# A hybrid decoder layer on one core: the output weights of cross-attention loaded into the queries' input room, the mixer's constants spread by DMA, the attention heads' buffers taken by the parity of the pair

## The chip, the core and the metric

The kernel runs on one core of one Trainium2 chip. A core has a matrix engine (PE, TensorE), three engines for elementwise work (DVE or VectorE, ACT or ScalarE, POOL or GpSimd) and SP (SyncE), which in this kernel only issues DMA transfers. Each engine carries out its own list of instructions in order and waits on semaphores for the others. The metric is the device time of one execution in microseconds, the median of several. The time includes a little before the first and after the last recorded instruction, so it is somewhat longer than the span of the trace.

## What is computed

One layer of a decoder over 1024 positions of 1024 channels, in float32, with three sub-layers. The reference, cut to its frame:

```python
h = rms_norm(x, g_pre_mix)
q, k, v, z, xbc, dt_raw, ga, gs = split(h @ w_in, IN_SIZES)
o_att = stick_breaking_attention(q, k, v)         # 16 heads of 64
o_ssm = ssd_branch(z, xbc, dt_raw, ...)           # Mamba-2: 32 heads of 64, 4 groups, state 128, chunks of 128
merged = sigmoid(ga) * (o_att @ w_br_att) + sigmoid(gs) * (o_ssm @ w_br_ssm)
x = x + rms_norm(merged @ w_mix_out, g_post_mix)
h = rms_norm(x, g_pre_xa)
mem_n = rms_norm(mem, g_mem)                      # 256 external memory rows
x = x + rms_norm(memory_cross_attention(h, mem_n, w_xq, w_xkv, w_xo), g_post_xa)   # 4 heads of 256
h = rms_norm(x, g_pre_ffn)
x = x + rms_norm(swiglu(h, w_gu, w_down), g_post_ffn)   # 2816 hidden
```

Stick-breaking attention weights position s for position t by exp(z_ts + the sum of log sigmoid(-z_tj) over j from s to t); the mixer's decays inside a chunk are exp of differences of a running sum a_cs, and 0 above the diagonal. The last product of cross-attention, `@ w_xo` with its norm and residual, is one of the two places that the change touches.

## The kernel before

**Numbers in two parts.** The matrix engine works here on a rounded float32 (fp32r). Each operand is therefore split into a high part (hi_sb, lines 88 to 97: a copy with rounding, on POOL by L93 or on ACT by L97, where no engine is named the two in turn) and a low part (lo_of, L99: what is left after subtracting the high part, L100, on DVE or POOL). Each product is three matmuls (mm3, L102 to 106): high by high (L103), high by low (L104), low by high (L105). A weight must so be loaded, rounded on one engine and subtracted on another before PE may use it.

**Stages.** In order of time: input projection; stick-breaking attention with the projections of its heads in between (to about 1080 us); the SSD mixer, with the memory's key and value projections mixed in; the two branch projections and the mixer's output projection; cross-attention; its output projection (1763 to 1890 us); the feed-forward layer and its down projection. A scheduler lays down each engine's order when the program is built, from the order in which the code asks for things, the free rooms of the buffer pools and its own idea of durations. What counts here is that the order on each engine is fixed: an instruction that waits holds all behind it on its engine, on SP too, where all DMA transfers stand in one list.

**Attention's end.** Heads are handled in pairs, hp from 0 to 7. ev_q and ev_k store the projected queries and keys of a pair into one tile per head, `qk` (queries, high keys, low keys), from a ring of four rooms: a new pair's two tiles take the rooms of the pair two earlier. PE computes scores (L867 to 883) into which DVE runs a scan (L882); then, for the values (L889 to 931), PE transposes the weights into one of three PSUM banks `tr` (L898), ACT makes their high part `wth` (L901), DVE the low part `wtl` (L902), which frees the bank, and PE multiplies both with the values (L910, L911). DVE multiplies the result with its gate (oT, L919), and SP stores it (o_d, L921) and a gate (g_d, L859).

**The memory.** While the last pairs are at work, SP loads the memory's gain (L1194) and its two blocks of 128 rows (L1199) into `wraw` tiles, a pool of three; ACT squares a block (L1201), POOL turns the mean into 1/root (rstd, L166 and L167), DVE normalises (L1202), and PE transposes (L1209). The `wraw` rooms are then used by the weights of the memory's keys and values (two_loads, L1218 to 1229, load L1225), high part on ACT, low part on DVE. These tiles lie in memory that attention's tiles had before, so the first of them wait for the last user of that memory.

**The mixer's decays.** A decay matrix of a chunk is one matmul (dec, L1077) of a row of `colrows` (128 x 8 heads x 128) with `keyrows` (128 x 512), followed by an exp on ACT (L1078). Rows 0 to 7 and 32 to 39 of both hold the heads' sums in two parts and the ones that select a head, rows 64 and 65 the sums of the columns; the others hold FAR = -2^120 times the identity against a mask of zeros and ones, so that what lies above the diagonal becomes exp of a huge negative number. There are two `colrows` and two `keyrows`, used in turn. What is constant in them is built once by DVE (L1015 to 1025): 128x1024 from the identity, then three narrow strips and two blocks of 8 rows for each `colrows`, and a copy of the mask for each `keyrows`. Of these sixteen, twelve go through `slow`, which pins each behind one of the last fourteen matmuls of the values, so that they are spread over attention's end. The sums that change from chunk to chunk are then loaded from DRAM: keyrows (L1033, called key_d below), colrows (L1070, sum_d), and the inputs xs (L1072).

**Cross-attention's output.** big_weight (L1334) loads a 1024x1024 weight in eight rows of tiles `raw` and makes eight tiles `bw`. Its `raw` tiles come from a ring of two `wraw` rooms, so a load waits until the low part of the weight two before it has been taken. For w_xo it is called on L1698 with npool = 2: the first two weights are done on POOL alone, the others get their high part by turns on POOL and ACT and their low part on DVE. out_proj (L1401) then runs over four row blocks, for each over the eight weights, into a PSUM tile `p`, one of two; ACT squares the result (L1417), DVE normalises it (L1419) and adds the residual (L1420). Cross-attention's queries are made from four `a8` tiles (128 x 2 x 1024) in the pool accp, which the queries' projection reads last; the same pool takes the FFN's input `hf` afterwards.

## Time and profile before

| what | us |
|---|---|
| median of 3 runs | 2546.85 (2546.82 to 2547.27) |
| the profiled execution's own time | 2547.56 |
| span of its trace | 2545.8 |
| mean granted clock of PE over the span | 0.995 |

The stages, from the busy table by stretch (PE's busy time):

| stretch, us | what runs | PE busy | share |
|---|---|---|---|
| 0 to 375 | input projection, first part | 356.9 | 95% |
| 375 to 680 | input projection, second part | 303.1 | 99% |
| 680 to 1080 | attention | 391.3 | 98% |
| 1080 to 1490 | mixer, memory's projections, first branch work | 394.4 | 96% |
| 1490 to 1760 | branch and output projections, cross-attention | 267.0 | 99% |
| 1760 to 1890 | cross-attention's end and its output projection | 126.5 | 97% |
| 1890 to 2546 | feed-forward, down projection | 635.9 | 97% |

A busy share is read as what is left over: where PE is busy for 97% of a stretch, 3% of it is all that other engines and transfers take from it, unless the granted clock is below 1, when the same matmuls take longer. In the rows quoted below, the columns of a list of single instructions are: start (us), length (us), engine, line, operation, written tile <- read tiles with shapes, count, and in brackets the idle time before it and what ended it. "SPq" is the instruction queue of SP, where a row is the issue of a transfer and not the transfer. A row of the list of waits gives engine, tile and line, then what ended the wait, then sum, count and longest in us.

### The profile page before, as it was taken

Reading aid. Unit: us, or ns where it says so; the run is one execution under the profiler, and the core shown is the slowest. Engines: PE = TensorE matmul, PEld = TensorE weight load, DVE = VectorE, ACT = ScalarE, POOL = GpSimd, SP = SyncE. Lnnn points to the kernel's source line nnn. Section 1 sums busy time; section 2 is a strip of 40 time slices with the busy share of each in tenths; the row PEclk is TensorE's granted clock in tenths of the full one; section 3 lists DMA queues with packets and bytes.
Section 4 is the critical chain, followed back from the end, with each engine's and each line's share of the span. In section 5 each row is a group of like instructions: output and inputs, shape, how many; then the busy total and the mean of one; then the engine's idle time right before and its main releaser. Section 6 shows DMA issues by size and latency. Waiting matters only on the chain. (4 is left out here: it accounts for less than half of the span.)

```text
span 2545.8 us, 32843 instructions
## 1 busy us (share of the span) xinstructions
PE 2475.0 (97%) x12002; PEld 2054.4 (81%) x12002; DVE 1858.3 (73%) x2205; ACT 1153.8 (45%) x2068; POOL 793.2 (31%) x632
## 2 busy tenths in 40 slices
PE   8999999999999999998999999999999999999998
PEld 6788788888888888787888788888787888887776
DVE  7685888776788887697888554576459666666997
ACT  6343455655555655565554302344233333334433
POOL 4331533321000000165655131131113233223675
PEclk9999999999999999999999999999999999999999
DMA  6441565445444454364332452311231322324322
GB/s 229 150 155 59 156 205 174 141 133 165 115 124 119 116 129 104 113 201 154 106 96 77 152 166 87 127 48 58 100 124 59 97 78 75 99 84 165 132 100 100
DMA packets 284524, 310.02 MB, mean 122 GB/s; under 512 B 17343, under 2 KB 204872, under 8 KB 283978
## 3 DMA queue, kind: packets, MB, share of 16 engines
q1 hardware_dynamic: 284362, 307.91, 39.0%
q8 instruction: 95, 1.56, 0.3%
q14 instruction: 67, 0.55, 0.1%
HBM read 206.26 MB, written 78.52 MB: 112 GB/s over the span
## 5 line engine op out<-in xcount | busy, mean ns | idle before, releaser
L882 DVE TENSOR_TENSOR_SCAN n<-n,mask 128x128 f32<-128x128 f32 (+7 forms) x128 | 170.7, 1349 | 37.9 <-ACT n L881 37.3
L199 POOL TENSOR_TENSOR sf<-wr,wr 128x512 f32<-128x512 f32 x38 | 59.3, 1561 | 351.1 <-DMA wr<-in_w_gu_dram 131.0
L100 DVE TENSOR_TENSOR sw<-sf,sw 128x512 fp32r<-128x512 f32 x150 | 116.3, 786 | 53.8 <-ACT sw L97 53.4
L93 POOL TENSOR_SCALAR whi<-wraw 128x1024 fp32r<-128x1024 f32 x10 | 18.4, 1836 | 398.5 <-PE mm L104 324.3
L97 ACT ACTIVATE sw<-sf 128x512 fp32r<-128x512 f32 x150 | 91.9, 624 | 95.1 <-PE mm L225 85.5
L881 ACT ACTIVATE n<-sc 128x512 f32<-128x512 f32 (+1 forms) x192 | 87.0, 493 | 93.3 <-PE sc L880 92.9
L225 PE MATMUL mm<-h,sw 128*128 128x512 f32 x320 | 124.3, 389 | 1.8 <-DVE sw L100 1.8
L97 ACT ACTIVATE sw<-wr 128x512 fp32r<-128x512 f32 x113 | 70.9, 629 | 121.0 <-PE mm L225 120.9
L223 PE MATMUL mm<-h,sw 128*128 128x512 f32 x320 | 122.4, 391 | 3.1 <-ACT h L97 2.3
L224 PE MATMUL mm<-h,sw 128*128 128x512 f32 x320 | 124.5, 389 | 0.0
L902 DVE SCALAR_TENSOR_TENSOR wtl<-tr,wth 128x512 fp32r<-128x512 f32 x192 | 99.5, 545 | 30.5 <-ACT wth L901 30.2
L901 ACT ACTIVATE wth<-tr,mone 128x512 fp32r<-128x512 f32 x192 | 106.6, 583 | 26.2 <-PE tr L898 24.1
L166 POOL TENSOR_SCALAR rstd<-ms 128x1 f32<-128x1 f32 x82 | 33.5, 409 | 262.6 <-ACT x L1417 101.8
L670 DVE SCALAR_TENSOR_TENSOR b<-b,prmT,b 128x1023 f32<-128x1023 f32 (+2 forms) x72 | 102.8, 1430 | 9.4 <-ACT b L668 8.9
L100 DVE TENSOR_TENSOR sw<-wr,sw 128x512 fp32r<-128x512 f32 x113 | 93.1, 827 | 18.9 <-ACT sw L97 18.8
L103 PE MATMUL mm<-oth,bw 128*128 128x512 f32 x256 | 103.6, 405 | 2.3 <-DVE a L1188 1.5
L898 PE MATMUL tr<-ident,n 128*128 128x128 f32 x576 | 98.7, 276 | 5.7 <-DVE wtl L902 5.7
L103 PE MATMUL p<-bw,h 128*128 128x512 f32 x256 | 99.4, 393 | 3.3 <-DVE x L1419 2.4
L105 PE MATMUL mm<-oth,bw 128*128 128x512 f32 x256 | 100.9, 394 | 0.0
L105 PE MATMUL p<-bw,h 128*128 128x512 f32 x256 | 100.5, 393 | 0.0
L104 PE MATMUL mm<-otl,bw 128*128 128x512 f32 x256 | 100.5, 393 | 0.0
L104 PE MATMUL p<-bw,h 128*128 128x512 f32 x256 | 100.4, 392 | 0.0
(695 smaller groups left out, 8182.6 us busy)
## 6 DMA issues: line engine op xcount, KB each, us to landing
wr<-in_w_gu_dram SPq DMA_DIRECT2D x80, 256.0 KB
wr<-in_w_in_dram SPq DMA_DIRECT2D x36, 512.0 KB
zr<-in_w_in_dram SPq DMA_DIRECT2D x32, 512.0 KB
gu_d<-t SPq DMA_DIRECT2D x44, 256.0 KB
qk<-hT SPq DMA_DIRECT2D x84, 128.0 KB
qk<-lT SPq DMA_DIRECT2D x84, 128.0 KB
wraw<-in_w_in_dram SPq DMA_DIRECT2D x20, 512.0 KB
b<-v_d SPq DMA_DIRECT2D x16, 512.0 KB
```

The source lines that it names most:

```text
L97: A.activation(o, i, AF.Copy)
L100: eng.tensor_tensor(o, i, hi.bitcast(F32), ALU.subtract)
L103: first = T.matmul(ps, sh, mh, start=start, stop=False)
L104: T.matmul(ps, sh, ml, start=False, stop=False)
L105: T.matmul(ps, sl, mh, start=False, stop=stop)
L223: T.matmul(ps, w[0][:, k, :], b[0][:, k, :], start=first and k == 0, stop=False, skip_group_check=True)
L224: T.matmul(ps, w[0][:, k, :], b[1][:, k, :], start=False, stop=False, skip_group_check=True)
L225: T.matmul(ps, w[1][:, k, :], b[0][:, k, :], start=False, stop=last and k == 3, skip_group_check=True)
L670: V.scalar_tensor_tensor(acc[:, sh:], y[:, :S - sh], cw(3 - sh, f), acc[:, sh:], ALU.mult, ALU.add)
L882: V.tensor_tensor_scan(nt[:, 0:L][:, ::-1], nt[:, 0:L][:, ::-1], mask[:, S - L:][:, ::-1], 1.0, ALU.mult, ALU.max)
L901: A.activation(wh[:, t0 * P:], pt[:, t0 * P:], AF.Identity, bias=mone)
L902: V.scalar_tensor_tensor(wl[:, t0 * P:], pt[:, t0 * P:], -1.0, wh[:, t0 * P:].bitcast(F32), ALU.add, ALU.subtract)
```

## The change

Three edits.

1. The heads' tiles `qk` come from two rings of two, `qk0` for even pairs and `qk1` for odd ones, in place of one ring of four. The room is the same.
2. The constants of the decays are no longer built in full by DVE. DVE makes one 128x128 tile `base` (four operations on at most 128x128), a DMA spreads it over the eight heads of colrows[0], DVE writes the two blocks of eight rows, a DMA copies colrows[0] into colrows[1], and two DMAs copy the mask into the two keyrows. Nothing of it is pinned any more.
3. big_weight can take its `raw` tiles from another pool. For w_xo these are the four `a8` tiles of accp, two weights in each, so that all eight loads have a room of their own. The six weights that POOL does not do alone now all get their high part on ACT.

```diff
--- before.py
+++ after.py
@@ -821,7 +821,7 @@
                     for j in range(2):
                         hd = heads[2 * hp + j]
                         if half == 0:
-                            t = mk(qk, [P, 3, S], F32R, "qk")
+                            t = mk(qk, [P, 3, S], F32R, f"qk{hp % 2}", bufs=2)
                             hd["q"], hd["kh"], hd["kl"] = [t[:, i] for i in range(3)]
                         q = hd["q"]
                         rows_ = slice(j * HD, (j + 1) * HD)
@@ -1002,26 +1002,21 @@
         HEADS, ONES = (0, 32), 64
         colrows = [mk(ep, [P, GH, P], F32R, f"colrows{i}") for i in range(NROW)]
         keyrows = [mk(ep, [P, HALF], F32R, f"keyrows{i}") for i in range(2)]
-        spread = iter(marks[-14:])
-
-        def slow(ins):
-            m = next(spread, None)
-            if m is not None:
-                issue_behind(ins, m)
-
+        base = mk(ep, [P, P], F32, "base")
+        V.tensor_scalar(base, ident, FAR, None, ALU.mult)
+        for r, n in ((0, GH), (32, GH), (ONES, 2)):
+            V.tensor_scalar(base[:, r:r + n], ident[:, r + n:r + n + 1].to_broadcast([P, n]), FAR, None, ALU.mult)
         u = mk(sm, [P, 4, P], F32, "cb")
         G.memset(u, 1.0)
         G.affine_select(u, u, [[0, 4], [1, P]], ALU.is_gt, 0.0, base=0, channel_multiplier=-1)
-        for t in colrows:
-            slow(V.tensor_scalar(t, ident.unsqueeze(1).to_broadcast([P, GH, P]), FAR, None, ALU.mult))
-            for r, n in ((0, GH), (32, GH), (ONES, 2)):
-                ins = V.tensor_scalar(t[:, :, r:r + n], ident[:, r + n:r + n + 1].unsqueeze(1).to_broadcast([P, GH, n]), FAR, None, ALU.mult)
-                if r != 32:
-                    slow(ins)
-            for r in HEADS:
-                slow(V.tensor_copy(t[r:r + GH], ident[r:r + GH, r:r + GH].unsqueeze(2).to_broadcast([GH, GH, P])))
+        t = colrows[0]
+        nc.sync.dma_start(t.bitcast(F32), base.unsqueeze(1).to_broadcast([P, GH, P]))
+        for r in HEADS:
+            V.tensor_copy(t[r:r + GH], ident[r:r + GH, r:r + GH].unsqueeze(2).to_broadcast([GH, GH, P]))
+        for i in range(1, NROW):
+            nc.sync.dma_start(colrows[i].bitcast(F32), t.bitcast(F32))
         for t in keyrows:
-            slow(V.tensor_copy(t, u.rearrange("p c i -> p (c i)")))
+            nc.sync.dma_start(t.bitcast(F32), u.rearrange("p c i -> p (c i)"))
             G.memset(t[ONES:ONES + 2].bitcast(F32), 1.0)
 
         def open_four(g, q):
@@ -1331,18 +1326,23 @@
 
 
 
-    def big_weight(wb, w, npool=0, rooms=()):
+    def big_weight(wb, w, npool=0, rooms=(), raws=None):
         wh, wl = [], []
         first = {}
         for k in rooms:
             first[k] = mk(wb, [P, D], F32, "wraw", bufs=2) if k is None else mk(wb, [P, 2, D], F32R, f"bw{k}", bufs=1)
         for k in range(KT):
-            raw = first.pop(None) if None in first else mk(wb, [P, D], F32, "wraw", bufs=2)
+            if raws is not None:
+                if k % 2 == 0:
+                    two = mk(raws, [P, 2, S], F32, "a8")
+                raw = two[:, k % 2]
+            else:
+                raw = mk(wb, [P, D], F32, "wraw", bufs=2)
             nc.sync.dma_start(raw, w[k * P:(k + 1) * P, :])
             both = first[k] if k in first else mk(wb, [P, 2, D], F32R, f"bw{k}", bufs=1)
             wh.append(both[:, 0, :])
             wl.append(both[:, 1, :])
-            hi_sb(wh[k], raw, "p" if k < npool else None)
+            hi_sb(wh[k], raw, "p" if k < npool else ("a" if raws is not None else None))
             lo_of(wl[k], raw, wh[k], G if k < npool else V)
         return wh, wl
 
@@ -1695,7 +1695,7 @@
     with ExitStack() as q3:
         gpool = pool(q3, "gx3")
         wbig = pool(q3, "wbigB", 8, side="right")
-        wxo = big_weight(wbig, a["w_xo"][0], 2, (7, 6, 5, 4, 3, None, 0, 1, 2))
+        wxo = big_weight(wbig, a["w_xo"][0], 2, (7, 6, 5, 4, 3, None, 0, 1, 2), accp)
         gpost, gpre = load_gain(gpool, "g_post_xa"), load_gain(gpool, "g_pre_ffn")
         hf = [quad(accp, "a8")]
         out_proj(0, ox[0], wxo, t4, psp, x2_d, x3_d, gpost, gpre, hf[0])
```

Behind the edit lines shift: between 1026 and 1330 a line of the changed kernel is the line of before less 5 (L1199 of before is L1194 of the changed one, L1225 is L1220, L1033 is L1028, L1070 is L1065); from 1341 on they are the same. Tile numbers differ between the two programs.

**How the order moves.** The first place is SP's list at the end of attention, where the memory's loads and the mixer's first loads stand; in brackets are the semaphores that an issue waits for (DMAHW is one of SP's eight earlier transfers, the rest are engines). Before:

```order
L1194 DMA wraw_10248<-in_g_mem_dram 128x1024 [waits DMAHW4_49,PE_49]
L1199 DMA wraw_10250<-in_mem_dram 128x1024 [waits DMAHW5_49]
L1199 DMA wraw_10258<-in_mem_dram 128x1024 [waits DMAHW6_49]
L1070 DMA colrows_2075_10224<-sum_d 1x8x128 [waits DMAHW7_49,DVE_49]
L921 DMA o_d<-oT_9745 128x512 [waits DMAHW0_49,DVE_49]
L859 DMA g_d<-gt_10098 128x512 [waits DMAHW1_49,Activation_49]
L1070 DMA colrows_2075_10224<-sum_d 1x8x128 [waits DMAHW2_49]
L1225 DMA wraw_10359<-in_w_xkv_dram 128x8x128 [waits DMAHW4_49,DMAHW3_49,DVE_49]
L1070 DMA colrows_2076_10225<-sum_d 1x8x128 [waits DVE_49]
L1035 DMA bfm_10296<-bf_d 128x512 [waits DMAHW5_49,PE_49]
L1037 DMA cfm_10298<-cf_d 128x512 [waits DMAHW6_49]
L1039 DMA btm_10300<-bt_d_64 128x4x128 [waits DMAHW7_49]
```

and then, a few rows on:

```order
L1033 DMA keyrows_2077_10226<-key_d 8x512 [waits DMAHW1_49,DVE_49]
L1033 DMA keyrows_2077_10226<-key_d 8x512 [waits DMAHW2_49]
L1072 DMA s_2101_10320<-xs_d_57 128x512 [waits DMAHW3_49]
L1033 DMA keyrows_2078_10227<-key_d 8x512 [waits DMAHW4_49,DVE_49]
L1033 DMA keyrows_2078_10227<-key_d 8x512 [waits DMAHW5_49]
L921 DMA o_d<-oT_9907 128x512 [waits DMAHW6_49,DVE_49]
L859 DMA g_d<-gt_10177 128x512 [waits DMAHW7_49,Activation_49]
L1072 DMA s_2108_10338<-xs_d_57 128x512 [waits DMAHW0_49]
L1039 DMA btm_10672<-bt_d_64 128x4x128 [waits DMAHW1_49]
L1225 DMA wraw_10363<-in_w_xkv_dram 128x8x128 [waits DMAHW2_49,PE_49]
```

In the changed kernel the first of these places reads:

```order
L1189 DMA wraw_10245<-in_g_mem_dram 128x1024 [waits DMAHW4_49]
L1194 DMA wraw_10247<-in_mem_dram 128x1024 [waits DMAHW5_49,PE_49]
L1013 DMA colrows_2075_10224<-base_10228 128x8x128 [waits DMAHW6_49,DVE_49]
L1194 DMA wraw_10255<-in_mem_dram 128x1024 [waits DMAHW7_49]
L921 DMA o_d<-oT_9745 128x512 [waits DMAHW0_49,DVE_49]
L859 DMA g_d<-gt_10098 128x512 [waits DMAHW1_49,Activation_49]
L1017 DMA colrows_2076_10225<-colrows_2075_10224 128x1024 [waits DMAHW6_49,DMAHW2_49,DVE_49]
L1065 DMA colrows_2075_10224<-sum_d 1x8x128 [waits DMAHW3_49,DMAHW2_49]
L1030 DMA bfm_10293<-bf_d 128x512 [waits DMAHW4_49,PE_49]
L1032 DMA cfm_10295<-cf_d 128x512 [waits DMAHW5_49]
L1034 DMA btm_10297<-bt_d_64 128x4x128
L1019 DMA keyrows_2077_10226<-cb_10233 128x512 [waits DMAHW7_49,Pool_49]
```

and goes on with

```order
L1028 DMA keyrows_2077_10226<-key_d 8x512 [waits DMAHW7_49,DMAHW4_49]
L859 DMA g_d<-gt_10177 128x512 [waits DMAHW5_49,Activation_49]
L921 DMA o_d<-oT_9907 128x512 [waits DMAHW6_49,DVE_49]
L1028 DMA keyrows_2077_10226<-key_d 8x512
L1065 DMA colrows_2076_10225<-sum_d 1x8x128 [waits DMAHW0_49]
L1067 DMA s_2109_10335<-xs_d_57 128x512 [waits DMAHW1_49]
L1220 DMA wraw_10356<-in_w_xkv_dram 128x8x128 [waits DMAHW2_49]
L1220 DMA wraw_10360<-in_w_xkv_dram 128x8x128 [waits DMAHW3_49,PE_49]
```

The gain (L1194, now L1189) no longer waits for PE, the first block of the memory does instead; the copy of `base` stands between the memory's two blocks. The first weights of the memory (w_xkv) stood ahead of the second store of oT and now stand behind it, as does the second half of key_d; xs now stands ahead of that store, not behind it.

The second place is DVE's list at the same time. Before:

```order
L882 SCALAR_TENSOR_TENSOR n_2035_10005<-n_2035_10005,mask_5575 128x1024
L1018 TENSOR_SCALAR colrows_2075_10224<-ident_88 128x8x8 x2
L1018 TENSOR_SCALAR colrows_2075_10224<-ident_88 128x8x2
L919 TENSOR_TENSOR oT_9745<-av_9999,gt_10040 64x512
L1018 TENSOR_SCALAR colrows_2076_10225<-ident_88 128x8x8
L1022 CAST colrows_2075_10224<-ident_88 8x1024 x2
L1202 SCALAR_TENSOR_TENSOR wraw_10250<-wraw_10250,rstd_10254,wraw_10248 128x1024
L1202 SCALAR_TENSOR_TENSOR wraw_10258<-wraw_10258,rstd_10262,wraw_10248 128x1024
L902 SCALAR_TENSOR_TENSOR wtl_10056<-tr_10050,wth_10055 128x512
L902 SCALAR_TENSOR_TENSOR wtl_10068<-tr_10062,wth_10067 128x512
L902 SCALAR_TENSOR_TENSOR wtl_10080<-tr_10074,wth_10079 128x512
```

In the changed kernel:

```order
L882 SCALAR_TENSOR_TENSOR n_2035_10005<-n_2035_10005,mask_5575 128x1024
L919 TENSOR_TENSOR oT_9745<-av_9999,gt_10040 64x512
L1015 CAST colrows_2075_10224<-ident_88 8x1024 x2
L1197 SCALAR_TENSOR_TENSOR wraw_10247<-wraw_10247,rstd_10251,wraw_10245 128x1024
L902 SCALAR_TENSOR_TENSOR wtl_10056<-tr_10050,wth_10055 128x512
L902 SCALAR_TENSOR_TENSOR wtl_10068<-tr_10062,wth_10067 128x512
L902 SCALAR_TENSOR_TENSOR wtl_10080<-tr_10074,wth_10079 128x512
L1197 SCALAR_TENSOR_TENSOR wraw_10255<-wraw_10255,rstd_10259,wraw_10245 128x1024
L902 SCALAR_TENSOR_TENSOR wtl_10092<-tr_10086,wth_10091 128x512
L902 SCALAR_TENSOR_TENSOR wtl_10107<-tr_10101,wth_10106 128x512
```

The two norms of the memory (L1202, now L1197) stood together ahead of the three low parts (L902) of the last values; the second now stands behind them. The wide constants of colrows are gone, the two casts of eight rows are left.

The third place is PE's list in the output projection, on one weight. Before, `bw_3310` is used for two row blocks, whose PSUM tiles are p_3325 and p_3334:

```order
L103 MATMUL p_3325_16431<-bw_3310_16389,h_3210_15984 128x512
L103 MATMUL p_3334_16511<-bw_3310_16389,h_3210_15984 128x512
L104 MATMUL p_3325_16431<-bw_3310_16389,h_3210_15984 128x512
L105 MATMUL p_3325_16431<-bw_3310_16389,h_3211_15985 128x512
L103 MATMUL p_3325_16431<-bw_3310_16389,h_3210_15984 128x512
L104 MATMUL p_3325_16431<-bw_3310_16389,h_3210_15984 128x512
L105 MATMUL p_3325_16431<-bw_3310_16389,h_3211_15985 128x512
L104 MATMUL p_3334_16511<-bw_3310_16389,h_3210_15984 128x512
```

In the changed kernel each weight is used for one block and PE goes on to the next weight:

```order
L103 MATMUL p_3323_16425<-bw_3311_16386,h_3211_15981 128x512
L104 MATMUL p_3323_16425<-bw_3311_16386,h_3211_15981 128x512
L105 MATMUL p_3323_16425<-bw_3311_16386,h_3212_15982 128x512
L103 MATMUL p_3323_16425<-bw_3311_16386,h_3211_15981 128x512
L104 MATMUL p_3323_16425<-bw_3311_16386,h_3211_15981 128x512
L105 MATMUL p_3323_16425<-bw_3311_16386,h_3212_15982 128x512
L103 MATMUL p_3323_16425<-bw_3307_16382,h_3211_15981 128x512
L104 MATMUL p_3323_16425<-bw_3307_16382,h_3211_15981 128x512
```

The second block follows when the first has gone through all eight weights.

## The prediction

> **What bounds the kernel now.** First the page: the share of each engine.
>
> ```profile
> span 2545.8 us, 32843 instructions
> PE 2475.0 (97%) x12002; PEld 2054.4 (81%) x12002; DVE 1858.3 (73%) x2205; ACT 1153.8 (45%) x2068; POOL 793.2 (31%) x632
> ```
>
> TensorE (PE) is busy for 2475.0 of 2545.8 us, so all engines together can win at most 70.8 us, and only where PE stands or runs at a lower clock. The change touches two places: the passage from the first attention to the SSD mixer (1040 to 1220 us) and the output projection of cross-attention (1763 to 1890 us). The list of PE's waits in windows around them names what can go.
>
> ```profile
> PE tr L898 <- DVE wtl L902: 2.6, 1, 2.6
> PE pst L103 <- ACT s2r L97: 2.5, 1, 2.5
> PE pst L103 <- ACT state L1099: 1.5, 1, 1.5
> PE dec L1077 <- ACT s L1078: 1.4, 1, 1.4
> ...
> PE p L103 <- DVE x L1419: 2.4, 1, 2.4
> ```
>
> A wait costs more than its length, as the busy table by stretch shows (columns: us, busy time of PE, PEld, DVE, ACT and POOL, granted clock, DMA share, GB/s).
>
> ```profile
> 1067.00:1070.00 3.00, 2.99 (x14) 2.50 (x15) 2.94 (x7) 0.69 (x1) 0.96 (x2) 0.69 0.61 176
> 1070.00:1074.00 4.00, 3.82 (x19) 3.05 (x18) 3.13 (x7) 2.79 (x6) 0.52 (x2) 0.81 0.66 198
> 1090.00:1220.00 130.00, 118.91 (x710) 102.74 (x709) 107.90 (x115) 75.84 (x140) 72.74 (x65) 0.99 0.53 161
> 1220.00:1400.00 180.00, 180.00 (x991) 154.27 (x990) 154.14 (x192) 92.02 (x180) 108.25 (x105) 1.00 0.32 94
> 1800.00:1810.00 10.00, 7.65 (x28) 5.91 (x27) 3.35 (x3) 2.26 (x4) 1.59 (x4) 0.83 0.13 53
> ```
>
> Behind the 2.6 us wait the clock is 0.69 and then 0.81: 3 x 0.31 + 4 x 0.19 = 1.7 us of work lost. Behind the 2.4 us wait it is 0.83 over 10 us, 1.7 us again. From 1220 us PE has no idle time at all, so what is won before it stays won.
>
> [...]
>
> **Part 1: heads' buffers by parity, constants by DMA.** The 2.6 us wait is the end of a chain that starts on SP, whose DMA queue stands for PE:
>
> ```profile
> SPq L1194 <- PE av L911: 4.5, 1, 4.5
> ...
> 1055.30 0.33 SPq L1194 DMA_DIRECT2D wraw<-in_g_mem_dram  x1
> ...
> 1060.87 1.06 ACT L1201 ACTIVATE junkm<-wraw 128x1024 bf16<-128x1024 f32 x1 [1.50 <-DMA wraw<-in_mem_dram]
> 1063.20 1.83 ACT L901 ACTIVATE wth<-tr,mone 128x512 fp32r<-128x512 f32 x3
> ...
> 1063.01 1.29 DVE L1202 SCALAR_TENSOR_TENSOR wraw<-wraw,rstd,wraw 128x1024 f32<-128x1024 f32 x1 [2.26 <-POOL rstd L167]
> 1065.07 1.28 DVE L1202 SCALAR_TENSOR_TENSOR wraw<-wraw,rstd,wraw 128x1024 f32<-128x1024 f32 x1 [0.77 <-POOL rstd L167]
> 1066.28 1.88 DVE L902 SCALAR_TENSOR_TENSOR wtl<-tr,wth 128x512 fp32r<-128x512 f32 x3
> ```
>
> The memory's gain waits until 1055.30 for a room of the last scores; the memory's rows land 1060.87 - 1055.30 = 5.6 us later; ScalarE (ACT) squares both ahead of three wth; VectorE (DVE) stands 2.26 and 0.77 us for rstd, does both norms, and only then the three wtl that free PE's transpose banks. In the changed order the gain waits for no matmul and the first memory row for an earlier head's scores, so both can go at 1055.3 - 4.5 = 1050.8 and land by 1056.4; ACT squares the first right behind its store of the gate at 1059.4; DVE's first norm can start at 1059.4 + (1063.01 - 1060.87) = 1061.5 and end at 1062.8. The second norm now stands behind the three wtl, and ACT's second square behind the three wth. The first wtl then ends near 1063.6, ahead of 1064.4, when PE would want it. The wait and its slow clock go: 2.6 + 1.7 = 4.3 us. What is late next is the fourth wtl, behind the second norm: ACT's square ends at about 1065, rstd and norm take 2.14 + 1.29, so it comes near 1068.5, some 0.5 us after PE's need. Part 1 gives 3.8 us.
>
> The constants themselves (columns: duration min/median/max in ns):
>
> ```profile
> L1016 DVE TENSOR_SCALAR colrows<-ident x2: 669/681/693, 1053.6 to 1055.3; 128x1024 fp32r<-128x1024 f32 x2
> L1018 DVE TENSOR_SCALAR colrows<-ident x6: 167/176/195, 1058.2 to 1068.2; 128x64 fp32r<-128x64 f32 x4, 128x16 fp32r<-128x16 f32 x2
> L1022 DVE CAST colrows<-ident x4: 675/682/1091, 1059.4 to 1069.7; 8x1024 fp32r<-8x1024 f32 x4
> L1024 DVE CAST keyrows<-cb x2: 417/418/420, 1073.2 to 1073.6; 128x512 fp32r<-128x512 f32 x2
> ```
>
> 2 x 0.68 + 6 x 0.18 + 4 x 0.68 + 2 x 0.42 = 6.0 us of DVE go; two casts (1.4 us) and four small ones on base (by the 0.18 us rows 0.7 us) remain: 3.9 us less. It is worth nothing directly, since DVE stood idle beside them, but nothing of it stands between wtl any more. Added are four DMAs, 1.5 MB. How long a copy inside SBUF takes no row shows. The nearest transfer with short pieces is a weight load of the mixer:
>
> ```profile
> 1095.59 0.38 SPq L1225 DMA_DIRECT2D wraw<-in_w_xkv_dram  x1
> ...
> 1099.90 1.06 ACT L97 ACTIVATE bw<-wraw 128x1024 fp32r<-128x1024 f32 x1 [2.55 <-DMA wraw<-in_w_xkv_dram]
> ```
>
> 512 KB take 4.3 us; the small sum rows and the 5.6 us above bound it from 1 to 6 us. I take 4.3. The copy of base can start at about 1054.4, when DVE has made base, and lands at 1058.7; DVE reaches the first cast at about 1058.9. Behind that cast stand the first norm and the wtl; the cover is the norm's rstd (1061.5, less 1.3 for the casts: 1060.2). Late beyond this, each us costs one.
>
> **The mixer's start.**
>
> ```profile
> 1074.24 0.33 PE L911 MATMUL av<-wtl,v 128*128 128x128 f32 x1 [0.42 <-DVE wtl L902]
> ...
> 1076.13 0.34 SPq L921 DMA_DIRECT2D o_d<-oT  x1
> ...
> 1076.12 0.48 PE L1077 MATMUL dec<-colrows,keyrows 128*128 128x512 f32 x1
> 1086.16 0.42 PE L103 MATMUL mm<-a,bw 128*128 128x256 f32 x1
> ```
>
> Attention would end at 1074.24 - 3.8 = 1070.4. On SP the second half of key_d and the first memory weights (xkv) now stand behind the store o_d, which follows attention's end by 1.9 us: o_d at 1072.3, key_d at 1072.8, landed between 1074 and 1077 (1 to 4.3 us), the first xkv at about 1074.3, landed at 1078.6, rounded on ACT by 1079.7. So the first dec waits some 2 us, the first memory matmul some 3 us more, and a slow clock may cost 1.7: 7 us. Gone are 2.5 + 1.5 + 1.4 us of waits, since xs no longer follows o_d, and their slow clock, again about 7. I put this at zero, between -3 (each landing at its long end) and +3 (each at its short one). From 1090 to 1220 PE idles 130 - 118.91 = 11.1 us beside a DVE that is busy for 83%; this may return or give up 2 us.
>
> **Part 2: the output weights.**
>
> ```profile
> 1763.89 28.52 SPq L1341 DMA_DIRECT2D wraw<-in_w_xo_dram  x8
> ...
> 1781.47 0.63 PE L103 MATMUL p<-bw,h 128*128 128x512 f32 x2
> ...
> 1782.16 1.05 ACT L97 ACTIVATE bw<-wraw 128x1024 fp32r<-128x1024 f32 x1
> 1782.91 2.35 DVE L100 TENSOR_TENSOR bw<-wraw,bw 128x1024 fp32r<-128x1024 f32 x2
> ...
> 1803.03 0.39 PE L105 MATMUL p<-bw,h 128*128 128x512 f32 x1
> 1802.32 1.03 ACT L1417 ACTIVATE x<-p 128x1024 f32<-128x1024 f32 x1 [3.73 <-PE p L105]
> 1804.43 1.28 DVE L1419 SCALAR_TENSOR_TENSOR x<-p,rstd,g_post_xa 128x1024 f32<-128x1024 f32 x1 [4.58 <-POOL rstd L167]
> ```
>
> The eight loads trickle over 28.5 us through two rooms, so PE runs two row blocks side by side on each weight as it comes. Both end at 1803.3, and the third block waits for the first one's bank until DVE's L1419 ends. With eight rooms all weights are there early. ACT then rounds six of them from 1782.2, one per 1.0 us, and DVE subtracts from 1783.2, one per 1.2 us (2.35 for two). PE does 18 matmuls on the first two weights, 18 x 0.227 = 4.1 us (96 matmuls from 1781.47 to 1803.26), and wants the third weight's low part at 1785.8: it is there at 1784.4, and each next one 1.2 us later against PE's 1.36. The first block ends at 1793.7; its bank is free 1804.43 + 1.28 - 1802.32 = 3.4 us after its square starts, by 1797.4, long before 1803.3. The wait and its slow clock go: 2.4 + 1.7 = 4.1, taken as 4.0; the bounds are 0 (DVE falls behind) and 4.1. Three roundings move from POOL to ACT, which is 45% busy; nothing waits there.
>
> **Sum.** 3.8 + 0 + 4.0 = 7.8 us. The profiled execution took 2547.56 us (span 2545.8), 0.7 above the median 2546.85; against the median this is 2539.1.
>
> **Rivals.** *One of the two only* (chance 0.25): the passage gives up its 3.8 us to the landings behind o_d, or DVE falls behind in part 2. Time 2546.85 - 4 = 2542.9, between 2541.8 and 2545.5.
>
> *POOL blocks DVE in cross-attention* (0.05). POOL now does its roundings as soon as the third head's scores have left the room, and its two subtractions beside DVE's normalisation:
>
> ```profile
> 1754.81 2.11 PE L1639 MATMUL p<-kT,qT 128*128 128x256 f32 x9
> ...
> 1760.60 1.23 DVE L1645 TENSOR_TENSOR prob<-prob,sm 128x1024 f32<-128x1024 f32 x1
> ...
> 1771.85 2.40 POOL L100 TENSOR_TENSOR bw<-wraw,bw 128x1024 fp32r<-128x1024 f32 x1
> ```
>
> If DVE stood for a whole subtraction, up to 2.4 us, the last softmax would be late by that and a clock loss of 1.7 could follow: 2539.1 + 4 = 2543. [...] No row of before has the two side by side; beside POOL's 2.40 us the other DVE rows keep their length.
>
> *Slower* (0.05): the memory weights come too late. ACT holds their rounding ahead of the mixer's exponentials, so PE's first memory matmul and all behind it wait. Before, PE got there at 1086.16; if the first weights are rounded later than that, the passage loses. With the 5.6 us landing three times in series behind 1074.24 (key_d, xs, xkv, as when 1.5 MB more share the queues) it is 1094, 8 us late: 2546.85 + 8 - 4 = 2551. *Nothing moves* (0.05): 2546.9, if DMA holds both.
>
> **Numbers.** The forecast, 2535 to 2541.7, has 0.60. Its own landings may be shorter (2535). 0.2%, or 5.1 us, is about what a measurement of this kernel can tell from no change. Faster by more (below 2541.75): 0.60 plus 0.06 from the edges of the rivals, 0.66. Within 0.2%: 0.29. Slower: 0.05. The range 2534.5 to 2545.5 leaves out the last two cases and a little of each edge.
>
> **What would show it.** The memory's gain issued near 1051 and no wait of PE for wtl above 0.6 us: part 1. PE's wait on dec under 3 us and the first memory matmul at about 1080: the passage. Loads of the output weights before 1760, no wait for L1419, granted clock 1.00 there: part 2. A DVE wait for the copy of base, or the first memory matmul after 1086, would make the prediction wrong.

## The result and the profile after

| | before | changed |
|---|---|---|
| median, us | 2546.82 (9 runs, 2544.41 to 2549.33) | 2540.46 (9 runs, 2537.07 to 2542.52) |
| ratio to before, 95% interval | | 0.9975 (0.9966 to 0.9984) |
| the profiled execution, us (span) | 2547.56 (2545.8) | 2542.52 (2540.8) |

The change makes the kernel 6.4 us faster, 0.25%; 2539.1 was predicted, so 1.4 us are missing. That is less than the interval of the ratio leaves open (2.3 us each way), so what is missing is read from the profiles below and not from the medians. The page of the changed kernel, the line on the engines that answers to that of before:

```profile
PE 2473.5 (97%) x12002; PEld 2053.7 (81%) x12002; DVE 1856.2 (73%) x2197; ACT 1156.7 (46%) x2071; POOL 791.5 (31%) x629
```

PE's work is the same; what went is waiting and low clock. PE's waits of the changed kernel, in one window for the passage (1040 to 1225 us) and in one for cross-attention and its output (1700 to 1900 us):

```profile
PE mm L103 <- ACT bw L97: 2.9, 1, 2.9
...
PE dec L1072 <- ACT cb L1048: 2.1, 1, 2.1
...
PE tr L898 <- DVE wtl L902: 0.3, 1, 0.3
...
PE mm L103 <- DVE h L1667: 1.8, 1, 1.8
```

Two waits are gone as forecast: wtl, 2.6 us before, is 0.3, and L1419, 2.4 us before, is missing. Two are new or longer: the memory's first weights (bw, 2.9) and h of cross-attention (1.8, where it was 1.1).

Two profiles are best compared by the same matmul. Each trace has 12002 matmul records; numbered in order of start, the time from one number to another can be set beside that of another kernel. Matmul 5200 starts at 1061.03 us of before, 5240 at 1072.99, 6000 at 1218.96, 8600 at 1753.30, 8680 at 1770.66, 8800 at 1796.45, 8840 at 1809.56. The same matmuls stand at the ends of each stretch in all kernels (in e_mx_act, whose cross-attention is ordered anew, nearly). All profiles of this case, in us:

```
                          5200 to   5240 to   8600 to   8680 to   8800 to
                             5240      6000      8680      8800      8840
                        attention   mixer's  cross-at-  first     the L1419
                          ends       start   tention   block         wait
before                      11.96    145.97     17.37     25.79     13.10
c_xo      (edit 3 alone)    11.65    144.19     18.76     25.80      9.07
a_parity  (edit 1 alone)     9.45    145.76     17.39     25.77     11.71
b_consts  (edit 2 alone)    11.62    145.22     17.37     25.79     11.71
changed                      7.69    147.47     18.75     25.78      9.07
after_again                  7.67    144.29     18.77     25.76      9.07
after_rounds                 7.67    142.18     19.10     27.02      9.07
d_first2                     7.69    142.04     17.37     25.75      9.07
d_again                      7.68    144.79     17.37     25.72      9.07
e_lo_dve                     7.67    141.90     17.37     29.75      9.07
e_mx_act                     7.67    142.23     18.56     25.73      9.07
f_raws_alt                   7.69    144.22     17.37     30.46      9.07
g_early                      7.68    149.38     17.37     25.75      9.07
```

after_again and after_rounds are the changed kernel itself, profiled again; the other names are the experiments below. In the two kernels that were profiled more than once (the changed one and that of d_first2), the columns of attention's end, of cross-attention and of the L1419 wait repeat within 0.4 us; the mixer's start does not, and the first block is 1.2 us longer in one of three profiles. Where two kernels have the same code in a stretch, the columns can be compared too: attention's end of before takes 11.62 to 11.96, but its L1419 wait takes 13.10 in one profile and 11.71 in two others (a_parity, b_consts).

### The profile page after: what moved, and what is told of

Its sections match the earlier page's. It is cut to its first block, busy times and chain, and to the rows that moved or that the text cites. A ratio compares the mean times of both kernels' runs of the same rounds, so it can differ in the third digit from the quotient of the medians.

```text
span 2540.8 us, 32839 instructions
## 1 busy us (share of the span) xinstructions
PE 2473.5 (97%) x12002; PEld 2053.7 (81%) x12002; DVE 1856.2 (73%) x2197; ACT 1156.7 (46%) x2071; POOL 791.5 (31%) x629
## 4 chain that ended last, share of the span: by engine, by line
PE 42%; DVE 6%; issue 1%; POOL 1%; DMA 1%; ACT 1%; SPq 0%; POOLq 0%; DVEq 0%; ACTq 0%
PE mm L225 5%; PE mm L223 5%; PE mm L224 5%; PE mm L103 4%; PE mm L104 4%; PE mm L105 4%; DVE op L100 2%; PE p L103 2%; PE p L104 2%; PE p L105 2%; PE pd L1124 2%; DVE a L1931 1%; PE p L1639 1%; DMA gr<-gu_d 1%; PE tr L181 0%
## 5 line engine op out<-in xcount | busy, mean ns | idle before, releaser
L902 DVE SCALAR_TENSOR_TENSOR wtl<-tr,wth 128x512 fp32r<-128x512 f32 x192 | 99.5, 545 | 29.8 <-ACT wth L901 29.4
L103 PE MATMUL p<-bw,h 128*128 128x512 f32 x256 | 99.7, 390 | 0.9 <-DVE m L1391 0.9
L100 DVE TENSOR_TENSOR zl<-zr,zh 128x512 fp32r<-128x512 f32 x84 | 75.4, 911 | 34.4 <-ACT zh L97 34.3
L105 PE MATMUL p<-bw,h 128*128 128x512 f32 x256 | 100.2, 392 | 0.0
```

Of the source, the lines that this page charges most:

```text
L100: eng.tensor_tensor(o, i, hi.bitcast(F32), ALU.subtract)
L103: first = T.matmul(ps, sh, mh, start=start, stop=False)
L105: T.matmul(ps, sl, mh, start=False, stop=stop)
L902: V.scalar_tensor_tensor(wl[:, t0 * P:], pt[:, t0 * P:], -1.0, wh[:, t0 * P:].bitcast(F32), ALU.add, ALU.subtract)
```

## Experiments

**1. The parity alone.**

```diff
-                            t = mk(qk, [P, 3, S], F32R, "qk")
+                            t = mk(qk, [P, 3, S], F32R, f"qk{hp % 2}", bufs=2)
```

> The first edit alone (the heads' tiles by parity); the order on every engine is that of before, only waits differ. Theory (the gain's wait for the last scores makes the norms late): the memory's gain is issued about 4 us earlier, ACT squares the first block from about 1059.4 instead of 1060.9, the norms come 1.5 us earlier, but both still stand ahead of the three wtl, so PE's wait for wtl (L898) falls from 2.6 to about 1.1 us and the time by 1.5 us, up to 3.2 if the slow clock behind the wait goes too: 2543.6 to 2545.3. Rival (the wait comes from the constants and the norms' place, not from the load): the wait stays at 2.6 us and the time at 2546.8.

Measured: 2544.38 us against 2546.0 of before on the same chip, ratio 0.9992 (0.9983 to 1.0001). SP, ACT and DVE of this kernel at the end of attention (all of its trace is 1.40 us later than that of before at this point, ACT's store of the gate at 1060.18 against 1058.78):

```profile
1052.28 0.42 SPq L1194 DMA_DIRECT2D wraw<-in_g_mem_dram  x1
...
1060.67 1.05 ACT L1201 ACTIVATE junkm<-wraw 128x1024 bf16<-128x1024 f32 x1
...
1062.93 1.28 DVE L1202 SCALAR_TENSOR_TENSOR wraw<-wraw,rstd,wraw 128x1024 f32<-128x1024 f32 x1 [0.78 <-POOL rstd L167]
1066.19 1.88 DVE L902 SCALAR_TENSOR_TENSOR wtl<-tr,wth 128x512 fp32r<-128x512 f32 x3
...
PE tr L898 <- DVE wtl L902: 1.8, 2, 1.5
```

The gain goes out at 1052.28 - 1.40 = 1050.9, not 1055.3, ACT squares at once, and the three wtl start at 1066.19 - 1.40 = 1064.8, 1.5 us earlier than before (1066.28). PE's wait is 1.8 in two parts, and no half clock follows: the stretch takes 9.45, 2.5 us less. In this stretch the theory holds in the middle of its range (1.5 to 3.2); the rival (load without effect) is out. The medians are 1.6 us apart, at the range's lower end, and their interval reaches 1.0001, so by themselves they would not show a gain.

**2. The constants by DMA alone** (the second hunk of the change: `base`, two casts, four DMAs).

```diff
-        for t in colrows:
-            slow(V.tensor_scalar(t, ident.unsqueeze(1).to_broadcast([P, GH, P]), FAR, None, ALU.mult))
...
+        nc.sync.dma_start(t.bitcast(F32), base.unsqueeze(1).to_broadcast([P, GH, P]))
...
+            nc.sync.dma_start(colrows[i].bitcast(F32), t.bitcast(F32))
```

> The second edit alone (constants by DMA). The gain still waits for the last scores, but the second norm stands behind the three wtl, and the first loads of the memory's weights behind the store of oT, as in the changed kernel. Theory (place and load each carry a part): the first norm ends at about 1064.3 as before, one norm less (1.28 us) stands ahead of wtl, so PE's wait for wtl falls from 2.6 to about 1.3 us; with the passage's landings at zero the time falls by 1.3 to 3 us: 2543.8 to 2545.5. Rival 1 (only the load counts): wait 2.6, time 2546.8. Rival 2 (only the place counts): the wait is gone, and this kernel alone wins the passage's whole 3.4 us: 2543.4.

Before, the constants are fourteen DVE instructions (2, 6, 4 and 2 in the rows of the prediction), not sixteen as the section on the kernel has it; six are left here, four of them small.

Measured: 2545.2 against 2546.0, ratio 0.9990 (0.9982 to 0.9999). In this kernel SP issues the copy of base behind the late gain, and DVE's first cast waits for it:

```profile
1055.78 0.33 SPq L1189 DMA_DIRECT2D wraw<-in_g_mem_dram  x1
1056.16 0.42 SPq L1194 DMA_DIRECT2D wraw<-in_mem_dram  x1
1056.68 0.67 SPq L1013 DMA_DIRECT2D colrows<-base  x1
...
1063.76 1.38 DVE L1015 CAST colrows<-ident 8x1024 fp32r<-8x1024 f32 x2 [4.31 <-DMA colrows<-base]
...
PE tr L898 <- DVE wtl L902: 2.6, 1, 2.6
```

The theory fell: PE's wait is 2.6 us as before, and attention's end takes 11.62. One norm less stands ahead of wtl, but DVE now stands 4.31 us for the copy, which took 1063.76 - 1056.68 = 7.1 us among the gain and the memory's two blocks, where the prediction had taken 4.3 (1 to 6) and named this cast as what a late copy would hold. It is rival 1 in its result, by a cause that neither rival has. In the changed kernel the gain and the first block have gone out earlier, and the cast finds its data there, 4.9 us after the copy's issue (1055.50 to 1060.35).

**3. The output weights alone** (the third hunk with its call; the high parts on ACT belong to it).

```diff
+            if raws is not None:
+                if k % 2 == 0:
+                    two = mk(raws, [P, 2, S], F32, "a8")
+                raw = two[:, k % 2]
...
-            hi_sb(wh[k], raw, "p" if k < npool else None)
+            hi_sb(wh[k], raw, "p" if k < npool else ("a" if raws is not None else None))
```

> The third edit alone (output weights into the queries' input room, high parts on ACT). Theory: PE's wait of 2.4 us for L1419 and the slow clock behind it go (4.0 us), but POOL's subtraction (L100, 2.35 us) again holds DVE's small TENSOR_SCALAR (L1641), which takes about 2.3 us instead of 0.17 while POOL subtracts, and PE's wait for h (L1667) is 0.7 us longer or more, 1.4 us lost in all: the time falls by 2.7 us, to 2544.1; up to 1060 us everything is as before. Rival (the loss there comes from the other two edits): L1641 takes 0.17 us and the whole 4.0 us are won: 2542.8.

Measured: 2544.09 against 2546.0, ratio 0.9988 (0.9979 to 0.9997). L1646 of this kernel is L1641 of before (columns: duration min/median/max in ns):

```profile
L1646 DVE TENSOR_SCALAR mx<-mx x8: 159/166/2275, 1675.6 to 1764.9; 128x4 f32<-128x4 f32 x8
```

One of eight takes 2.28 us, the stretch of cross-attention is 18.76 instead of 17.37, and the L1419 stretch 9.07 instead of 13.10: 4.03 won, 1.39 lost, as in the changed kernel. Both belong to the third edit. Together that is 2.6 us, and the medians are 1.9 apart.

**4. The first two weights late.** The loss was to go if POOL's subtraction no longer meets the softmax:

```diff
-            if raws is not None:
+            if raws is not None and k >= npool:
```

> The changed kernel, but the first two output weights, which POOL does alone, are loaded through the two old rooms, so late as in the kernel before (landing near 1769), the other six early as in the change. Theory (POOL's subtraction holds DVE's L1641): POOL works behind the last softmax, every L1641 takes 0.16 to 0.17 us, PE's wait for h (L1667) is 1.1 us again instead of 1.8, and 1.4 us are won: 2540.5 becomes 2539.1; out_proj starts without a wait and its first block still runs alone. Rival (the loss comes from the early transfers or from the order): L1641 is short, but the wait for h stays at 1.8 us and the time at 2540.5. Rival 2: POOL ends after 1780 and PE waits for the first weights: slower than 2540.5.

Measured: 2537.21 against 2546.0, ratio 0.9963 (0.9950 to 0.9977). POOL's first subtraction in this kernel, DVE's L1641, and PE's wait:

```profile
1764.08 2.40 POOL L100 TENSOR_TENSOR bw<-wraw,bw 128x1024 fp32r<-128x1024 f32 x1
...
L1641 DVE TENSOR_SCALAR mx<-mx x8: 158/165/171, 1670.1 to 1758.0; 128x4 f32<-128x4 f32 x8
...
PE mm L103 <- DVE h L1667: 1.1, 1, 1.1
```

POOL works behind the last softmax, every L1641 is short, cross-attention takes 17.37 again, and the 4.03 stay. The theory is confirmed; its 1.4 us are seen in the stretch. The median is the lowest of all versions; how it stands against the changed kernel is told under 9.

**5. POOL's subtractions on DVE.**

```diff
-            lo_of(wl[k], raw, wh[k], G if k < npool else V)
+            lo_of(wl[k], raw, wh[k], G if k < npool and raws is None else V)
```

> The changed kernel with POOL's two subtractions (L100) for the first two output weights put on DVE, at the end with the other six; POOL keeps the two roundings (L93). Theory (POOL's subtraction blocks DVE's small TENSOR_SCALAR): every L1641 takes 0.16 to 0.17 us, PE's wait for h (L1667) is 1.1 us instead of 1.8, 1.4 us are won there; DVE has eight subtractions of 1.2 us to do instead of six when out_proj begins, so PE waits up to 2 us there: the total between 2539 and 2541. Rival (the roundings or the early loads delay the softmax): one L1641 still takes about 2.3 us.

Measured: 2539.37 against 2547.08, ratio 0.9970 (0.9960 to 0.9980). POOL's roundings still stand beside the softmax, and L1641 is 0.17 us at most: cross-attention takes 17.37. So the loss comes with the subtraction; the early loads and the roundings where they stand do not bring it. Whether a rounding would hold L1641 is not shown, since none meets it in time: both stand beside L1640, which keeps its 1.22 us. The first block then takes 29.75, 4.0 more: PE waits 2.1 us for DVE's weights, and a half-clock window follows. By the stretches this version should be 2.6 us slower than the changed kernel; the medians do not show it (7.7 us under before, against 6.4 and 6.9), and as one wait was followed by half clock in one profile and not in others (13.10 and 11.71 in the column of L1419), 1.7 of the 4.0 may be missing in other executions.

**6. The small scaling on ACT.**

```diff
-            V.tensor_scalar(mx, mx, -sc, None, ALU.mult)
+            A.activation(mx, mx, AF.Copy, scale=-sc)
```

> The changed kernel with the small scaling of the maxima (L1641, 128x4) on ACT in place of DVE; POOL's subtractions stay where they are. Theory (DVE's TENSOR_SCALAR is what POOL's subtraction blocks, while DVE instructions that read PSUM pass): no DVE instruction between 1754 and 1762 takes longer than its form does elsewhere, and ACT's exponentials begin without a wait of 2 us; the time is within 1.5 us of 2540.5, since the order of cross-attention is laid down anew. Rival (any DVE instruction is blocked, whichever is next): another DVE instruction beside POOL's first subtraction is longer by some 2 us.

Measured: 2538.48 against 2547.08, ratio 0.9971 (0.9960 to 0.9982). DVE and POOL of this kernel around POOL's subtractions:

```profile
1752.80 1.22 DVE L1640 TENSOR_REDUCE mx<-p 128x4 f32<-128x1024 f32 x1
1754.16 0.69 DVE L1667 TENSOR_TENSOR h<-mm,h 128x512 fp32r<-128x512 f32 x1 [0.15 <-ACT h L1666]
1756.25 0.18 DVE L1644 RECIPROCAL sm<-sm 128x4 f32<-128x4 f32 x1 [1.39 <-ACT prob L1643]
1756.46 2.59 DVE L1645 TENSOR_TENSOR prob<-prob,sm 128x1024 f32<-128x1024 f32 x1
...
1753.27 4.69 POOL L100 TENSOR_TENSOR bw<-a,bw 128x1024 fp32r<-128x1024 f32 x2
```

The theory was half right. L1640 and L1667, which read PSUM, pass beside POOL in their usual time, and so does the reciprocal of 128x4. But L1645, with two operands in SBUF, takes 2.59 instead of 1.23 us: it is held until POOL's pair ends at 1757.96, and PE's wait for h is 2.3. So L1641 is not the only instruction of DVE that POOL's pair holds up.

**7. High parts by turns again.**

```diff
-            hi_sb(wh[k], raw, "p" if k < npool else ("a" if raws is not None else None))
+            hi_sb(wh[k], raw, "p" if k < npool else None)
```

> The changed kernel with the high parts of the six later output weights by turns on POOL and ACT again, as in the kernel before; only POOL's and ACT's lists differ. Theory (the early loads carry the whole gain, the move to ACT none): PE's list and waits are the same, the block still begins without a wait; POOL does three more roundings behind its two subtractions from about 1760.7 on, beside the last softmax; if a rounding blocks DVE's small TENSOR_SCALAR too, one L1641 more takes up to 1 us and PE's wait for h grows by 0.5: 2540.5 to 2541.5. Rival (ACT is needed): PE waits for a weight in the first block, over 1 us.

Measured: 2541.48 against 2547.08, ratio 0.9982 (0.9972 to 0.9992). POOL's list now has five roundings ahead of its two subtractions. Here are the last of them, the subtractions, and DVE's six beside them:

```profile
1777.06 1.05 POOL L93 TENSOR_SCALAR bw<-a 128x1024 fp32r<-128x1024 f32 x1 [8.11 <-PE mm L104]
1778.07 5.67 POOL L100 TENSOR_TENSOR bw<-a,bw 128x1024 fp32r<-128x1024 f32 x2
...
1778.81 10.55 DVE L100 TENSOR_TENSOR bw<-a,bw 128x1024 fp32r<-128x1024 f32 x6 [0.25 <-ACT bw L97]
...
PE p L104 <- POOL bw L100: 2.8, 1, 2.8
```

The theory fell, the rival holds. The roundings wait for rooms that cross-attention still uses, and the subtractions of the first two weights stand behind them. There they also meet DVE's subtractions, and both engines lose by it: DVE's six take 10.55 us instead of 6.90 in the changed kernel, POOL's two 5.67 instead of 4.69. PE waits 2.8 us, with half clock behind it (1.7 us of the loss): the first block takes 30.46, 4.7 more than in the changed kernel. Being late, the subtractions no longer meet the softmax (17.37), so 3.3 us are lost in all (the medians are too close to show it). The move to ACT is worth about that in this profile, not for ACT's time but because it takes waiting instructions out of POOL's list; how the 4.7 divide between the late start and the meeting with DVE was not tested.

**8. The changed kernel, profiled again.**

> The changed kernel itself, a second profile. Theory (half clock comes in windows of 3.41 us that follow a grid window in which PE was busy for less than about 48%, and the grid stands differently to the program in each execution): the waits are the same within 0.3 us, but half-clock windows stand elsewhere, and the 6000th matmul starts up to 3.4 us earlier or later against the 5200th than in the first profile. Rival (the slow windows belong to the kernel): half clock again at 1081.8 and twice behind 1204.7, and the two profiles agree within 0.3 us.

Measured: 2538.57 us. The mixer's start took 144.29 instead of 147.47 us. Where the first profile has half clock twice behind 1204.7, this one has it once; that is 1.7 of the 3.2 us. The rival is out, but the theory holds only in part: the waits are not the same within 0.3 us (bw 2.4 instead of 2.9, the three for pd together 1.3 instead of 2.1). Of the other 1.5 us most is idle time of PE (16.8 us in the stretch against 15.5). Single profiles of this stretch differ by 3 us and more.

**9. The changed kernel and the kernel with late first weights, side by side.**

> The changed kernel, timed beside the next two on the same chip. Expected about 6.5 us under the kernel before, with POOL's subtraction again beside one L1641 of 2.3 us and PE's wait for h at 1.8 us, whatever the half-clock windows do elsewhere.

> The kernel whose first two output weights come late, again. Theory (1.4 us from POOL's subtraction): 1.4 us under the changed kernel of this call, within 1 us; the first profile's larger lead in the mixer (half-clock windows missed by luck) does not return. Rival (the late loads win more than that, elsewhere): 3 us or more under the changed kernel.

Measured, before at 2546.62: the changed kernel 2539.72, ratio 0.9972 (0.9963 to 0.9981); with late first weights 2537.63, ratio 0.9964 (0.9952 to 0.9977). The difference, 2.1 us, is of the expected size, but the intervals of the two ratios overlap; what carries the claim is the column of cross-attention, 18.75 to 19.10 in three profiles of the one and 17.37 in two of the other. In after_rounds the 1.8 us wait also brought a half-clock window, so that the first block is 1.2 us longer as well.

**10. The memory's weights ahead of the last store.**

```diff
+                ld = nc.sync.dma_start(raw.rearrange("p (k f) -> p k f", k=k), src)
+                if st["n"] == 1:
+                    issue_behind(stores[-1], ld)
```

> The kernel with late first weights, and the last store of oT pinned behind the first load of the memory's weights, which so no longer waits for attention's end. Theory (the landings behind o_d cost PE a wait of 1.4 to 2.9 us for bw and 1.1 to 1.4 us for key_d): both waits shrink to under 1 us each and the start of the memory's matmuls comes 1 to 3 us earlier, the time 1 to 3 us under the kernel with late first weights. Rival (something else of the mixer's start is late next: the table load on ACT, the decays' exp, or xs): the two waits shrink, but as much comes back before 1130 us and the time stays within 1 us.

Measured: 2539.89 against 2546.62, ratio 0.9976 (0.9967 to 0.9985), 2.3 us behind the kernel it started from, though the intervals of the two ratios overlap. PE's waits of this kernel in the passage:

```profile
PE pd L1124 <- DVE s L1127: 3.7, 3, 2.1
...
PE dec L1072 <- DMA keyrows<-key_d: 2.3, 1, 2.3
...
PE dec L1072 <- ACT s L1073: 2.0, 2, 1.5
...
PE mm L103 <- ACT bw L97: 0.9, 1, 0.9
```

The wait for bw shrinks from 1.4 (d_first2) to 0.9, but the one for key_d grows from 1.1 to 2.3, those for the decays too, and the mixer's start takes 149.38. The theory fell: the weights are no longer late, but the keys and the decays are. The lists of much of the mixer differ from those of the kernel it started from, and this profile has five half-clock pieces in the stretch where those of d_first2 and d_again have three and two, so which of these waits costs how much is not settled.

## Why the prediction was right

**Bounds and place.** The gain came from the two waits that were named, and the part won before 1220 us stayed won up to cross-attention: from matmul 6000 to 8600 PE takes 534.34 us before and 533.69, 533.33 and 534.53 in the three profiles of the changed kernel.

**Part 1: 3.8 predicted, 4.3 measured.** The steps can be checked one by one. The first profile of the changed kernel is 1.34 us late at this point (the gate's store: the first row is of before, the others of the changed kernel); less that, its rows stand beside the prediction's times:

```profile
1058.78 0.60 ACT L858 ACTIVATE gt<-mm 128x512 f32<-128x512 f32 x1 [2.23 <-issue]
...
1060.12 0.60 ACT L858 ACTIVATE gt<-mm 128x512 f32<-128x512 f32 x1 [2.23 <-issue]
1060.62 1.05 ACT L1196 ACTIVATE junkm<-wraw 128x1024 bf16<-128x1024 f32 x1
...
1052.22 0.42 SPq L1189 DMA_DIRECT2D wraw<-in_g_mem_dram  x1
...
1060.35 1.38 DVE L1015 CAST colrows<-ident 8x1024 fp32r<-8x1024 f32 x2
1062.75 1.28 DVE L1197 SCALAR_TENSOR_TENSOR wraw<-wraw,rstd,wraw 128x1024 f32<-128x1024 f32 x1 [1.02 <-POOL rstd L167]
...
1070.77 0.33 PE L911 MATMUL av<-wtl,v 128*128 128x128 f32 x1
...
1081.95 0.58 PE L103 MATMUL mm<-a,bw 128*128 128x256 f32 x1 [2.94 <-ACT bw L97]
```

| step | predicted | measured, less 1.34 |
|---|---|---|
| gain issued | 1050.8 | 1050.9 |
| first cast on DVE | 1058.9 | 1059.0, without a wait |
| first square on ACT | 1059.4 | 1059.3 |
| first norm on DVE | 1061.5 | 1061.4 |
| attention ends | 1070.4 | 1069.4 |
| first memory matmul | about 1080 | 1080.6 |

Against the other two profiles with 2.6 us of wait (11.62, 11.65) it is 3.9 to 4.0. The 0.5 us kept for the fourth wtl came to 0.3, and the last matmul's own wait of 0.42 went with it. What the prediction did not see is how the two edits need each other: the parity alone gives 2.5 of the 4.3, the constants alone 0.3, since their copy then collides with the late memory loads.

**The mixer's start: 0 (-3 to +3) predicted.** The order of before takes 145.97 and 144.19, and 145.76 with edit 1; the new order, in the three profiles of the changed kernel and the five others that keep it (d to f), 141.90 to 147.47, on average 143.6. That is 1.7 less, inside the range, with a spread of 5.6 between executions, so neither size nor sign is settled by it. b_consts, which has the passage's new order but the late loads, takes 145.22. The landings were as described: o_d waits for attention, the weights come behind it, PE waits 2.9, 2.4 and 1.4 us for them in the three profiles. Of the three waits that were to go, those of 2.5 and 1.5 us for s2r and state are gone from pst, and the one of 1.4 us for s is 1.0 us in the first profile.

**Part 2: 4.0 predicted, 4.03 measured** in the L1419 stretch of the profiled pair. The steps hold: eight loads are issued in 4.5 us from 1707.8 on (1763.89 before; this trace runs 2.1 us ahead here), six roundings and subtractions run back to back, and the first block ends without a wait for a weight.

```profile
L1341 SPq DMA_DIRECT2D a<-in_w_xo_dram x8: 327/424/455, 1707.8 to 1711.8; - x8
...
1781.47 5.79 ACT L97 ACTIVATE bw<-a 128x1024 fp32r<-128x1024 f32 x6
...
1782.56 6.90 DVE L100 TENSOR_TENSOR bw<-a,bw 128x1024 fp32r<-128x1024 f32 x6 [0.26 <-ACT bw L97]
```

Only the 1.7 us of slow clock in it are less firm than the text made them: in a_parity and b_consts the same wait is followed by no half clock, and the stretch takes 11.71. Against such an execution part 2 is worth 2.6.

**The step that failed** is the sum's choice between the forecast and the rival "POOL blocks DVE in cross-attention". It was given 0.05 and a price of 4; it took place in every profile of the changed kernel, beside the gain of part 2, and costs 1.4 us. In the first profile of it, POOL, DVE and ACT:

```profile
1755.99 4.69 POOL L100 TENSOR_TENSOR bw<-a,bw 128x1024 fp32r<-128x1024 f32 x2
...
1756.13 2.27 DVE L1641 TENSOR_SCALAR mx<-mx 128x4 f32<-128x4 f32 x1
...
1758.43 0.47 ACT L1643 ACTIVATE prob<-p,mx 128x256 f32<-128x256 f32 x1 [2.04 <-DVE mx L1641]
```

A scaling of 128x4, 0.17 us elsewhere, ends with POOL's first subtraction, ACT's exponentials wait 2.04 us for it, and the last softmax and PE's h are late. Before the change POOL's subtractions ran from 1771.85 on, when DVE had only PSUM readers left; the early loads brought them forward by 16 us, 14 without this trace's lead. The prediction had named the place, the engine and what frees it. The instruction that was held is another than the one it named: the scaling L1641 ahead of the exponentials, not the normalisation L1645 behind them. It argued from "no row of before has the two side by side", which is no evidence when the change is what brings them there; and the DVE rows beside POOL's 2.40 us that keep their length all read PSUM (L1667, L1656).

The trace of before had better evidence in another stage. In the feed-forward layer L1730 multiplies two SBUF tiles, sometimes while POOL's L202 runs:

```profile
L1730 DVE TENSOR_TENSOR t<-t,t x20: 683/1659/1668, 1959.3 to 2311.1; 128x512 f32<-128x512 f32 x20
...
2028.81 1.67 DVE L1730 TENSOR_TENSOR t<-t,t 128x512 f32<-128x512 f32 x1
...
2028.18 1.75 POOL L202 TENSOR_TENSOR sf<-wr,sf 128x512 f32<-128x512 f32 x1
```

The sixteen that stand beside L202 take 1.66 us, the four beside which POOL does nothing 0.69. With such rows in view, 0.05 was too small a chance for the rival. (For an instruction with one SBUF operand the trace of before has a single case: one of the four casts of L1022 takes 1.09 us instead of 0.68, beside POOL's L1014.)

With that term the sum is 7.8 - 1.4 = 6.4 us, and 2546.82 - 2540.46 = 6.4 were measured; that it fits so closely is partly chance, as the mixer's spread shows: the spans of the two first profiles are 5.0 apart.

**High parts on ACT** were costed at nothing. That they add no wait on ACT is right; but the loads alone would not have been enough, as PE then waits 2.8 us for POOL (experiment 7).

## What to carry to other kernels

When a transfer is brought forward, look at what its arrival sets off: here an engine off the critical path worked 14 us earlier and held VectorE (2.27 us for a scaling of 0.17) at the one place where that counted, so the version with the lowest median loads early what ACT and DVE prepare late, and late what POOL prepares. A copy that replaces engine work has to be placed in the queue as carefully as the work in its list, since here one took 7 us behind other loads and held an engine for 4. An edit that gains next to nothing alone (0.3 us at attention's end) can be worth more beside another (1.8); test the pair before dropping one.
